# A two-layer encoder kernel with dense expert products: fewer tokens in the dense V product, more row groups, a shorter top-k table and a product moved to ScalarE

## The chip, the cores and the metric

One core of one Trainium2 chip. Its engines run side by side: TensorE (PE in the profile; PEld is its weight load), VectorE (DVE), ScalarE (ACT), GpSimd (POOL) and the DMA queues, which SyncE (SP) and POOL feed. The metric is the device time of one execution in microseconds, and the median of several.

## The reference

A trunk of two layers over 272 tokens (256 and 16 meta tokens), 1024 wide, all in float32. Layer 0 mixes tokens with a gated recurrence, layer 1 with a convolution. After each mixer comes the channel mixer that this document is about: per layer 16,384 experts with a row of U and a row of V each, of which every token uses 8 heads x 16.

```python
def peer_block(xc, w_query, sub_keys, expert_u, expert_v):
    q = (xc @ w_query).reshape(c, PEER_HEADS, 2, PEER_HALF)
    scores = jnp.einsum('chpk,pnk->chpn', q, sub_keys.astype(q.dtype))
    s1, i1 = lax.top_k(scores[:, :, 0], PEER_TOPK)
    s2, i2 = lax.top_k(scores[:, :, 1], PEER_TOPK)
    cand = (s1[..., :, None] + s2[..., None, :]).reshape(c, PEER_HEADS, PEER_TOPK * PEER_TOPK)
    s, flat = lax.top_k(cand, PEER_TOPK)
    ...
    g = jax.nn.softmax(s.astype(jnp.float32), axis=-1).astype(xc.dtype)
    act = jax.nn.gelu(jnp.einsum('chkd,cd->chk', expert_u[expert], xc))
    return jnp.einsum('chk,chkd->cd', g * act, expert_v[expert])
```

16 keys of 128 are picked on each of two axes, their 256 sums are made, and the best 16 sums are the experts. The last layer normalization drops the meta tokens, so layer 1 works on 256 tokens.

## The kernel before

**Dense, not gathered.** For most tokens `peer` computes all 16,384 experts: 128 tiles of U (128 experts each) times the tokens, GELU, a weight that is zero for experts that the token did not pick, and 128 tiles of V. `DENSE_U` gives the tokens for which U is dense (240 in both layers), `DENSE_V` those for which V is (208 and 192). Each loaded tile (512 KB, `raw`) is split into a rounded part `hi` (ScalarE, `load_split`, L159) and the rest `lo` (VectorE or POOL, L168), and a U tile is 24 matmuls in three passes: hi by the tokens' high part, hi by their low part, lo by the high part (`linears`, L196; tile `xs`). A V tile is eight matmuls by hi on both parts of the weights at once (L797) and eight by lo (L801).

**Few groups.** The other tokens are worked in groups of 16, which are 16 tokens x 8 heads = 128 rows. For pick k, `few_rows` gathers one row per partition by an indirect DMA from POOL's queue; `few_mult` takes the dot with x on VectorE, `few_add` adds a weighted row of V to `few_out`. A group outside DENSE_U needs 16 dots and 16 row sums (`EARLY`, `LATE`). A `DRAWN` group lies inside DENSE_U: POOL copies its dense results to a table in DRAM (`few_dump`) and fetches the picked ones (`few_draw`). At the end of a group TensorE adds `few_out` to the V sums (L843, 16 records). `near` groups take their expert positions from the main selection by way of DRAM (`few_spread`, `few_fetch`, on SP's queue); the group at 256 has a selection of its own (`few_topk`, in layer 0 alone).

**Stages of a layer.** First the query products and the scores, then:
- U, tiles 0 to 63 (`u_store` per tile). Meanwhile VectorE selects: 16 keys per axis and head, the table `cand`, the best 16 of it, positions, one-hot look-up of the keys (`topk_steps`). The tokens from 128 on are selected first. The selection of tokens 0 to 127 (`slow`) runs up to its heads' scans right behind, and its last eight steps between U tiles. POOL makes lo for tiles below `LO_FROM` = 34, VectorE from there. From `DOTS_FROM` = 41 on, 14 dots of the early group.
- U, tiles 64 to 127, with the gates (`u_out`). Chunks of 8 tokens: `one_hot` builds, on VectorE, a one-hot matrix of the first key (A) and of the second key times the high and the low half of the softmax weight (Bh in place, and Bl); `g_unit` multiplies them on TensorE (16 matmuls, L722 and L723) into the weights of all experts, and `weigh` multiplies these into the stored GELUs. Row groups go on: 2 dots, 8 row sums.
- V, 128 tiles. `few_plan` spreads the remaining row operations over tiles 4 to 112 by costs (3 for a row of an early group, 2 for the others); 72 row operations in layer 0, 56 in layer 1.

The order on each engine is set by a scheduler that keeps each engine's program order except where `issue_after` pins an instruction behind another. The buffers: lo 2, raw 4 and hi 2, and one `spare` that serves raw or hi (`self.fifth`).

Of the kernel before, what the change touches and what calls it, by code (L numbers as in the profile page):

```python
# [64 lines left out]
class Trunk:  # L65
# [514 lines left out]
    def peer(self, layer, n, xs):  # L580
# [10 lines left out]
        with tc.tile_pool(name=f"few{layer}", bufs=1) as kp:  # L591
            iT = ip.tile([HK, n // HC, 2, HC, 2], F16, name="iT")
            ghT = ip.tile([HK, n, 2], F16, name="ghT")
            glT = ip.tile([HK, n, 2], F16, name="glT")
            act_a = ap0.tile([P, JA, nu], F32, name="act_a")

            with tc.tile_pool(name=f"top{layer}", bufs=1) as sp:
# [7 lines left out]
                early, late, drawn = ([self.few_new(kp, layer, t0) for t0 in g[layer]] for g in (EARLY, LATE, DRAWN))  # L605
                near = [few for few in early + late + drawn if few["t0"] < 2 * P]
                for c0, md in ctiles:
# [8 lines left out]
                    if c0:  # L616
                        picked.append((c0, md, *self.topk(sp, sc, P)))
                        for few in early + late:
                            self.few_turn(sp, few, xs)
# [9 lines left out]
                def u_store(j, ps):  # L629
                    self.fifth = True  # L630
                    if j == LO_FROM:
                        with tc.issue_after(self.last_load):
                            self.few_load(kp, early[0], "kept")
                    behind = [few for few in early if few.get("left")]
                    if j >= LO_FROM and behind:
                        with tc.issue_after(self.dve_lo.ins):
                            for _ in range(min(2, behind[0]["left"])):
                                self.few_picked(behind[0])
                    elif j >= LO_FROM and len(picked[-1]) == 2:
# [38 lines left out]
            with tc.tile_pool(name=f"act1{layer}", bufs=1) as ap1:  # L678
# [16 lines left out]
                def one_hot(c0):  # L695
                    pairs = [HK, HC, NK // 2, 2]

                    def spread(t):
# [5 lines left out]
                    nc.vector.tensor_tensor(AB.rearrange("p x c (a b) -> p (x c) a b", b=2), keys,  # L704
# [758 lines left out]
```

## Time and profile before

| | us |
|---|---|
| median of 3 runs (1751.38 to 1758.8) | 1755.71 |
| the profiled execution | 1746.11 |
| its span | 1744.3 |
| layer 0: U 0 to 63, gates, V | 172.8, 350, 547 to 860 |
| layer 1: U 0 to 63, gates, V | 1055, 1231, 1428 to 1733 |

The last two rows give where in the span the stages begin, read from TensorE's timeline. A matmul's duration in the profile overlaps the next one's, so a tile's time is the distance between starts. In the timelines a bracket gives the idle time before an instruction and who ended it.

### The profile page before, as it was taken

Reading aid. Unit: us, or ns where it says so; the run is one execution under the profiler, and the core shown is the slowest. Engines: PE = TensorE matmul, PEld = TensorE weight load, DVE = VectorE, ACT = ScalarE, POOL = GpSimd, SP = SyncE. Lnnn points to the kernel's source line nnn. Section 1 sums busy time; section 2 is a strip of 40 time slices with the busy share of each in tenths; the row PEclk is TensorE's granted clock in tenths of the full one; section 3 lists DMA queues with packets and bytes.
Section 4 is the critical chain, followed back from the end, with each engine's and each line's share of the span. In section 5 each row is a group of like instructions: output and inputs, shape, how many; then the busy total and the mean of one; then the engine's idle time right before and its main releaser. Section 6 shows DMA issues by size and latency. Waiting matters only on the chain.

```text
span 1744.3 us, 34681 instructions
## 1 busy us (share of the span) xinstructions
PE 1716.3 (98%) x13436; PEld 1673.5 (96%) x13436; DVE 1507.6 (86%) x2818; ACT 899.6 (52%) x1491; POOL 616.1 (35%) x422
## 2 busy tenths in 40 slices
PE   8999999999999999999999999999999999999997
PEld 7899999999999999999989899999999999999997
DVE  7785998899997899988689869978889988889876
ACT  5553544554445555786542545445454455555553
POOL 1101892210202556752000017932102217777410
PEclk9999999999999999999999999999999999999999
DMA  5536667876757999998632356579767669999984
GB/s 206 169 134 183 182 198 262 299 236 194 228 183 232 340 360 373 364 373 322 208 122 72 121 175 170 182 254 318 243 191 221 219 202 326 335 363 353 344 310 153
DMA packets 126022, 423.83 MB, mean 243 GB/s; under 512 B 20768, under 2 KB 21920, under 8 KB 125728
## 3 DMA queue, kind: packets, MB, share of 16 engines
q1 hardware_dynamic: 96272, 324.04, 56.5%
q0 software_dynamic: 29584, 97.58, 15.2%
q8 instruction: 105, 1.72, 0.4%
q14 instruction: 61, 0.50, 0.1%
HBM read 411.35 MB, written 10.20 MB: 242 GB/s over the span
## 4 chain that ended last, share of the span: by engine, by line
PE 47%; DVE 3%; ACT 1%; DMA 0%; POOL 0%; issue 0%; DVEq 0%; ACTq 0%; POOLq 0%; SPq 0%
PE u L196 22%; PE acc L797 11%; PE acc L801 7%; PE u L243 3%; PE cv L1337 2%; PE g L722 1%; PE g L723 1%; DVE lo L168 0%; PE pre L263 0%; PE sps L613 0%; PE acc L843 0%; PE var L932 0%; DMA raw<-pw 0%; POOL lo L168 0%; ACT hi L159 0%
## 5 line engine op out<-in xcount | busy, mean ns | idle before, releaser
L159 ACT ACTIVATE hi<-raw 128x1024 fp32r<-128x1024 f32 x554 | 586.5, 1059 | 566.7 <-PE acc L797 241.9
L168 DVE TENSOR_TENSOR lo<-raw,hi 128x1024 fp32r<-128x1024 f32 x486 | 594.0, 1223 | 142.7 <-ACT hi L159 140.7
L196 PE MATMUL u<-xs,hi 128*128 128x240 f32 (+2 forms) x4544 | 569.0, 277 | 0.7 <-DVE xs L415 0.6
L196 PEld LDWEIGHTS u<-xs,hi 128*128 128x128 f32 x4544 | 537.6, 189 | 1.8 <-DVE xs L415 1.0
L797 PE MATMUL acc<-w,hi 128*128 128x416 f32 (+1 forms) x1952 | 401.2, 347 | 0.9 <-ACT hi L159 0.9
L797 PEld LDWEIGHTS acc<-w,hi 128*128 128x128 f32 x1952 | 339.8, 189 | 2.2 <-ACT hi L159 1.0
L1092 POOL DMA_INDIRECT rows<-peer_v,ids x128 | 203.0, 1586 | 313.1 <-DVE few_out L1133 168.9
L196 PE MATMUL u<-xs,lo 128*128 128x240 f32 (+2 forms) x2272 | 307.7, 276 | 4.1 <-POOL lo L168 4.0
L196 PEld LDWEIGHTS u<-xs,lo 128*128 128x128 f32 x2272 | 280.7, 189 | 6.0 <-POOL lo L168 5.6
L801 PEld LDWEIGHTS acc<-w,lo 128*128 128x128 f32 x2016 | 262.6, 191 | 0.9
L801 PE MATMUL acc<-w,lo 128*128 128x208 f32 (+1 forms) x2016 | 263.2, 272 | 0.0
L168 POOL TENSOR_TENSOR lo<-raw,hi 128x1024 fp32r<-128x1024 f32 x68 | 176.9, 2622 | 103.6 <-PE u L196 72.0
L1133 DVE SCALAR_TENSOR_TENSOR few_out<-rows,act,few_out 128x1024 f32<-128x1024 f32 x120 | 153.8, 1281 | 5.5 <-DMA rows<-peer_v,ids 5.4
L1092 POOL DMA_INDIRECT rows<-u_rows,ids x48 | 61.2, 1276 | 177.6 <-DVE rows L1099 134.1
L1109 POOL DMA_INDIRECT act<-own,turn x80 | 111.2, 1391 | 27.5 <-issue 18.6
L243 PE MATMUL u<-x,raw 128*128 128x272 f32 x480 | 114.1, 398 | 5.1 <-DMA x<-h 5.1
L243 PEld LDWEIGHTS u<-x,raw 128*128 128x128 f32 x480 | 92.5, 193 | 24.5 <-DMA raw<-w_in 5.1
L729 ACT ACTIVATE act_b<-g 128x488 f32<-128x488 f32 (+39 forms) x50 | 19.4, 389 | 116.9 <-DVE act_b L691 91.7
L407 POOL TENSOR_SCALAR xs<-x,par 128x272 fp32r<-128x272 f32 (+1 forms) x4 | 3.5, 878 | 180.5 <-DVE x L393 180.5
L704 DVE TENSOR_TENSOR AB<-iota,iT 128x2048 f16<-128x2048 f16 x50 | 61.1, 1225 | 0.0
L1099 DVE SCALAR_TENSOR_TENSOR rows<-rows,wide 128x1024 f32<-128x1024 f32 x48 | 58.5, 1219 | 1.1 <-DMA rows<-u_rows,ids 0.9
L778 POOL COPY own<-act_b 128x512 f32<-128x512 f32 (+2 forms) x15 | 14.6, 979 | 120.5 <-ACT act_b L740 94.3
(301 smaller groups left out, 1807.7 us busy)
## 6 DMA issues: line engine op xcount, KB each, us to landing
raw<-peer_u SPq DMA_DIRECT2D x256, 512.0 KB, 4.2
raw<-peer_v SPq DMA_DIRECT2D x248, 512.0 KB, 6.2
raw<-w_query SPq DMA_DIRECT2D x28, 512.0 KB, 3.8
raw<-pw SPq DMA_DIRECT2D x22, 512.0 KB, 3.5
raw<-w_in SPq DMA_DIRECT2D x16, 512.0 KB, 4.3
raw<-w_out SPq DMA_DIRECT2D x8, 512.0 KB, 3.9
raw<-peer_v SPq DMA_DIRECT2D x16, 256.0 KB, 4.5
own<-own POOLq DMA_DIRECT2D x15, 256.0 KB, 4.8
```

The lines of the kernel that those rows point to most:

```text
L159: self.act_hi = nc.scalar.activation(hi, raw, AF.Copy).ins
L168: i = e.tensor_tensor(lo[:, s], raw[:, s], hi[:, s].bitcast(F32), op=OP.subtract)
L196: self.mm = nc.tensor.matmul(ps[:, :n], l[:, k, :], xs(k, r)[:, :n], start=start, stop=stop)
L243: self.mm = self.nc.tensor.matmul(ps[:, :n], raw[:, k, :], x[:, k, :n], start=k == 0, stop=k == NB - 1)
L704: nc.vector.tensor_tensor(AB.rearrange("p x c (a b) -> p (x c) a b", b=2), keys, iT[:, c0 // HC].rearrange("p x c b -> p (x c) b")[:, :, N ...
L797: self.mm = nc.tensor.matmul(acc[b][:, :2 * n].rearrange("p (a t) -> p a t", a=2), hi, w[:, :, :n], start=j == 0, stop=j == NK - JG - 1, s ...
L801: self.mm = nc.tensor.matmul(main[b][:, :n], hi if p_ else lo, w[:, i, :n], start=False, stop=j == NK - 1 and not p_, skip_group_check=True)
L1092: self.last_rows = self.nc.gpsimd.indirect_dma_start(out=t, out_offset=None, in_=table, in_offset=bass.IndirectOffsetOnAxis(ap=few["ids"][ ...
L1099: self.nc.vector.scalar_tensor_tensor(t, t, 1.0, few["x"], op0=OP.mult, op1=OP.mult, accum_out=few["act"][:, k:k + 1])
L1109: self.nc.gpsimd.indirect_dma_start(out=few["act"][:, k:k + 1], out_offset=None, in_=few["table"].rearrange("p j (t o) -> (p j t) o", o=1) ...
L1133: nc.vector.scalar_tensor_tensor(few["out"], t, w, few["out"], op0=OP.mult, op1=OP.add)
L1337: nc.tensor.matmul(ps[:, :m], diag[i, b, k], h[j][:, s + k:s + k + m], start=(i, j, k) == steps[0], stop=False)
```

## The change

1. `DENSE_U` becomes (240, 224) and `DENSE_V` (192, 176). In both layers there are two early groups (240 and 256 in layer 0, 240 and 224 in layer 1) and three drawn ones; `LATE` goes. 80 tokens in layer 0 and 80 in layer 1 now have V from rows (64 before).
2. U tiles 0 to 63 hold 22 dots (from tile 29), the gate stage the other 10, all 16 row sums of the first early group and 4 of the second; V has 60 row operations in each layer. The first group's sum goes to DRAM and comes back in V (`few_spill`, `reload`). The rows of the gate stage alternate between a buffer of their own and `spare`, so raw has 4 buffers there.
3. VectorE takes lo from tile 25. The last eight steps of `slow` are at the tiles in `SLOW`.
4. `cand` keeps the sums of the first 4 keys with all 16 and of the other 12 with the first 4: 112. Four more small operations turn a place in it into the two positions. The look-up adds in a tree instead of a reduction.
5. Bl is made by ScalarE, one instruction per token with a scale per partition, and the A and B matrices of a chunk are built right behind the gate before.

```diff
-DENSE_U, DENSE_V = (240, 240), (208, 192)
-EARLY, LATE, DRAWN = ((256,), (240,)), ((240,), ()), ((224, 208), (224, 208, 192))
-DOTS_FROM, DOTS, ROWS, AHEAD, LO_FROM = 41, 14, 8, 2, 34
+DENSE_U, DENSE_V = (240, 224), (192, 176)
+EARLY, DRAWN = ((240, 256), (240, 224)), ((224, 208, 192), (208, 192, 176))
+DOTS_FROM, DOTS, ROWS, AHEAD, LO_FROM = 29, 22, 4, 2, 25
+SLOW = (25, 26, 27, 28, 30, 32, 34, 36)
+NEAR = 4
...
-SPREAD = 21
+SPREAD = 18
...
-        hi = self.stream("hi", F32R, 2, not self.fifth)
+        hi = self.stream("hi", F32R, 2, self.fifth is False)
...
-                    nc.vector.tensor_tensor(Bl_, Bh_, spread(glT), op=OP.mult)
-                    nc.vector.tensor_tensor(Bh_, Bh_, spread(ghT), op=OP.mult)
+                    for c in range(HC):
+                        nc.scalar.activation(Bl[:, c], Bh[:, c], AF.Copy, scale=glT[:, c0 + c:c0 + c + 1])
+                    hot["gate"] = Bh.rearrange("p c (a b) -> p c a b", b=2), ghT[:, c0:c0 + HC, None, :].to_broadcast(pairs)
...
+                    Bh_, gates = hot.pop("gate")
                     with tc.issue_after(second[0]):
-                        one_hot(c0)
+                        nc.vector.tensor_tensor(Bh_, Bh_, gates, op=OP.mult)
...
+                    if c0 + CC < n:
+                        with tc.issue_after(i.ins):
+                            one_hot(c0 + CC)
...
+                ops = later + [(first, 1, k) for k in range(TOPK)] + [(second_, 1, k) for k in range(ROWS)]
+                for e, (few, i, k) in enumerate(ops):
+                    t = e * (NK - JA - 7) // len(ops) + (2 if i and few is second_ else 0)
+                    home = (rp, "rows") if e % 2 else (self.wp, "spare")
+                    at_tile(t, self.few_rows, home[0], few, i, k, 1, home[1], order=False)
+                    at_tile(t + 3, *((self.few_add, few, k, kp, "kept") if i else (self.few_mult, few, k)))
...
-        cand = sp.tile([P, H, K, K], F32, tag=f"cand{H}", name="cand", bufs=1)
-        nc.vector.tensor_tensor(cand[:m], sv[:m, :, 0, :, None].to_broadcast([m, H, K, K]),
-                                sv[:m, :, 1, None, :].to_broadcast([m, H, K, K]), op=OP.add)
+        cand = sp.tile([P, H, NEAR * K + (K - NEAR) * NEAR], F32, tag=f"cand{H}", name="cand", bufs=1)
+        for part, rows, cols in ((cand[:m, :, :NEAR * K], slice(0, NEAR), slice(0, K)),
+                                 (cand[:m, :, NEAR * K:], slice(NEAR, K), slice(0, NEAR))):
...
-            nc.vector.tensor_reduce(idx[:m].rearrange("p a h k -> p (a h) k")[:, g:g + w], oh[:m, g:g + w],
-                                    op=OP.add, axis=AX.X)
+            for o in (8, 4, 2):
+                nc.vector.tensor_tensor(oh[:m, g:g + w, :, :o], oh[:m, g:g + w, :, :o], oh[:m, g:g + w, :, o:2 * o], op=OP.add)
+            nc.vector.tensor_tensor(idx[:m].rearrange("p a h k -> p (a h) k")[:, g:g + w], oh[:m, g:g + w, :, 0],
+                                    oh[:m, g:g + w, :, 1], op=OP.add)
...
-        rows = [(few, i, k) for few in early + late + drawn for i in range(2)
-                for k in range((ROWS if few in early else 0) if i else 0 if few in late else TOPK, TOPK)]
+        first, second = early
+        rows = [(second, k) for k in range(ROWS, TOPK)] + [(few, k) for few in drawn for k in range(TOPK)]
```

VectorE's program in layer 0, where its selection ends and lo begins (`fi<-fv` are the scans of a head's sums; `lo` is that of U tile 34). Before:

```order
L970 MAX fv<-r_2076 128x8
L971 MAX_INDEX fi<-fv,r_2076 128x8
L168 TENSOR_TENSOR lo<-raw,hi 128x1024
L974 CAST s_3209<-si 128x32
L977 TENSOR_SCALAR pu<-fi 128x16
L978 TENSOR_SCALAR pu<-fi 128x16
L980 CAST pf<-pu 128x64
L987 TENSOR_TENSOR oh<-iota_98,pf 128x512
L168 TENSOR_TENSOR lo<-raw,hi 128x1024
```

And now, where this `lo` is that of tile 25 and the steps of `slow` follow (`far` and `pu` are the small operations on the places):

```order
L997 MAX fv<-r_2094 128x8
L998 MAX_INDEX fi<-fv,r_2094 128x8
L170 TENSOR_TENSOR lo<-raw,hi 128x1024
L1001 CAST s_2941<-si 128x256
L1006 TENSOR_SCALAR far<-fi 128x128
L1007 TENSOR_SCALAR pu<-fi 128x128
L1008 TENSOR_SCALAR far<-far 128x128
L1009 TENSOR_SCALAR pu<-fi 128x128
L1010 TENSOR_TENSOR pu<-pu,far 128x128
L1011 SCALAR_TENSOR_TENSOR pu<-pu,fi 128x128
L1013 CAST pf<-pu 128x512
L170 TENSOR_TENSOR lo<-raw,hi 128x1024
```

The first lo of VectorE still stands behind the last scan, but belongs to a tile nine earlier, and the main selection's steps come straight behind it.

VectorE in the gate stage of layer 0, one chunk: `act_a<-g` and `act_b<-g` are the weighings, `AB<-iota` the one-hots of the next chunk but one, `AB<-AB,ghT` the high product of the next. Before:

```order
L691 SCALAR_TENSOR_TENSOR act_a<-g,act_a 128x64x8
L691 SCALAR_TENSOR_TENSOR act_b<-g,act_b 128x24x8
L711 TENSOR_TENSOR Bl<-AB,glT 128x1024
L704 TENSOR_TENSOR AB<-iota,iT 128x2048
L712 TENSOR_TENSOR AB<-AB,ghT 128x1024
L168 TENSOR_TENSOR lo<-raw,hi 128x1024
L744 TENSOR_TENSOR act_b<-act_b,tmp 128x80
L168 TENSOR_TENSOR lo<-raw,hi 128x1024
```

And now:

```order
L699 SCALAR_TENSOR_TENSOR act_a<-g,act_a 128x64x8
L699 SCALAR_TENSOR_TENSOR act_b<-g,act_b 128x15x8
L1133 SCALAR_TENSOR_TENSOR rows,act_1625<-rows,wide 128x1024
L710 TENSOR_TENSOR AB<-iota,iT 128x2048
L726 TENSOR_TENSOR AB<-AB,ghT 128x1024
L170 TENSOR_TENSOR lo<-raw,hi 128x1024
L755 TENSOR_TENSOR act_b<-act_b,tmp 128x48
L170 TENSOR_TENSOR lo<-raw,hi 128x1024
L755 TENSOR_TENSOR act_b<-act_b,tmp 128x48
```

Bl is gone from VectorE; in this chunk a dot of a row group stands in its place, in others none.

ScalarE in the same stage (`act_b<-u` and `tmp` are the GELUs of a U tile). Before:

```order
L159 ACTIVATE hi<-raw 128x1024
L740 ACTIVATE act_b<-u 128x152
L743 ACTIVATE tmp<-u 128x88
L729 ACTIVATE act_b<-g 128x36x8
L159 ACTIVATE hi<-raw 128x1024
```

And now:

```order
L161 ACTIVATE hi<-raw 128x1024
L751 ACTIVATE act_b<-u 128x152
L754 ACTIVATE tmp<-u 128x88
L715 ACTIVATE Bl<-AB,glT 128x128 x8
L740 ACTIVATE act_b<-g 128x34x8
L161 ACTIVATE hi<-raw 128x1024
```

The eight low products of the next chunk stand between a tile's GELUs and the rest of the gate's weighing, ahead of the next hi.

More of the change, by code (lines that the diff above doesn't have):

```diff
@@ L604, in peer @@
                 picked = []
-                early, late, drawn = ([self.few_new(kp, layer, t0) for t0 in g[layer]] for g in (EARLY, LATE, DRAWN))
-                near = [few for few in early + late + drawn if few["t0"] < 2 * P]
+                early, drawn = ([self.few_new(kp, layer, t0) for t0 in g[layer]] for g in (EARLY, DRAWN))
+                near = [few for few in early + drawn if few["t0"] < 2 * P]
+                dots = [(few, 0, k) for few in early for k in range(TOPK)]
+                dots, later = dots[:DOTS], dots[DOTS:]
                 for c0, md in ctiles:
@@ L617, in peer @@
                         picked.append((c0, md, *self.topk(sp, sc, P)))
[L618 removed]
+                        for few in early:
                             self.few_turn(sp, few, xs)
@@ L630, in u_store @@
                     self.fifth = True
-                    if j == LO_FROM:
+                    if j in (LO_FROM, SLOW[-1]):
                         with tc.issue_after(self.last_load):
-                            self.few_load(kp, early[0], "kept")
+                            self.few_load(*((sp, early[0], "turned") if j == LO_FROM else (kp, early[1], "kept")))
                     behind = [few for few in early if few.get("left")]
[L635 to L639, printed above, removed]
+                    if j in SLOW:
                         with tc.issue_after(self.dve_lo.ins):
@@ L789, in peer @@
                 vp = row_pool.__enter__()
-                self.few_plan(kp, vp, early, late, drawn, scale)
+                self.fifth = True
+                self.few_plan(kp, vp, early, drawn, scale)
                 acc = [self.bank(NB - 1 - b, f"acc{b}") for b in range(NB)]
@@ L1111, in few_draw, with few_spill @@
             in_offset=bass.IndirectOffsetOnAxis(ap=few["turn"][:, k:k + 1], axis=0))
-    def few_gelu(self, few, last):
-        self.nc.scalar.activation(few["act"], few["act"], AF.Gelu_apprx_tanh)
-        if last:
-            self.warm(AF.Abs_reciprocal_sqrt)
+    def few_spill(self, few):
+        few["sum"] = self.dp.tile([P, D], F32, name=f"sum{few['layer']}_{few['t0']}")
+        self.nc.gpsimd.dma_start(few["sum"], few["out"])
     def few_load(self, pool, few, tag):
@@ L1142, in few_plan, with reload @@
         begin = 4
         slots = len(rows) + ahead
-        cost = list(accumulate(3 if few in early else 2 for few, _, _ in rows + rows[-1:] * ahead))
+        cost = list(accumulate(3 if few is second else 2 for few, _ in rows + rows[-1:] * ahead))
         at = [begin + (c - cost[0]) * (NK - 4 * JG - begin) // cost[-1] for c in cost]
+        def reload():
+            first["out"] = vp.tile([P, D], F32, tag="wide", name="few_out", bufs=1)
+            with self.tc.issue_after(self.last_load):
+                self.nc.sync.dma_start(first["out"], first["sum"])
@@ L1147, in step @@
         def step(s):
-            if s == ahead and not late:
+            if s == ahead:
                 self.warm(AF.Abs_reciprocal_sqrt)
             if s >= ahead:
-                few, i, k = rows[s - ahead]
-                if i == 0:
-                    self.few_mult(few, k)
-                    if k == TOPK - 1:
-                        self.few_gelu(few, few is late[-1])
-                else:
-                    if k == 0:
-                        self.few_weigh(few, scale)
-                    self.few_add(few, k, *few["home"])
-                    if k == TOPK - 1:
-                        self.sums.append((at[s] + 4, few))
@@ L1162, in step @@
-            if s < len(rows):
-                few, i, k = rows[s]
-                if i == 0 and "loaded" not in few:
-                    few["loaded"] = self.few_load(vp, few, "wide")
-                few["rows"][k] = self.few_rows(vp, few, i, k, ahead + 1)
-        self.steps = [(t, lambda s=s: step(s)) for s, t in enumerate(at)]
+                few, k = rows[s - ahead]
+                if k == 0:
+                    self.few_weigh(few, scale)
+                self.few_add(few, k, *few["home"])
@@ L1173, in few_plan @@
         self.steps.sort(key=lambda s: s[0])
-        self.sums = []
+        self.sums = [(begin + 1, first)]
     def few_step(self, j):
```

111 lines of the change are left out of this document (63 added, 48 removed).

## The prediction

> **What bounds the kernel now.** I read the page's busy shares and chain first, then the windows by stage, then single tiles in the timelines.
>
> ```profile
> PE 1716.3 (98%) x13436; PEld 1673.5 (96%) x13436; DVE 1507.6 (86%) x2818; ACT 899.6 (52%) x1491; POOL 616.1 (35%) x422
> PE 47%; DVE 3%; ACT 1%; DMA 0%; POOL 0%; issue 0%; DVEq 0%; ACTq 0%; POOLq 0%; SPq 0%
> ```
>
> TensorE is busy 98% of the span and is nearly all of the chain that names an engine. The stages (columns: stretch, length, busy PE, PEld, DVE, ACT, POOL, clock, DMA share, GB/s) are, for each layer, the first half of U, the second half of U with the gates, and V:
>
> ```profile
> 176.00:352.00 176.00, 173.84 (x1540) 172.75 (x1539) 163.07 (x466) 88.79 (x140) 102.16 (x49) 1.00 0.74 238
> 352.00:546.00 194.00, 193.47 (x1919) 192.50 (x1918) 182.69 (x267) 94.16 (x215) 25.02 (x23) 1.00 0.65 207
> 548.00:848.00 300.00, 298.98 (x1997) 296.43 (x1996) 260.76 (x280) 192.10 (x290) 154.19 (x108) 1.00 0.94 343
> 1056.00:1233.00 177.00, 174.79 (x1548) 173.60 (x1547) 155.71 (x451) 88.17 (x138) 100.89 (x49) 1.00 0.74 237
> 1233.00:1426.00 193.00, 192.75 (x1892) 191.52 (x1891) 177.55 (x257) 93.70 (x212) 35.82 (x31) 1.00 0.67 211
> 1428.00:1720.00 292.00, 292.00 (x2054) 291.83 (x2053) 244.73 (x267) 156.71 (x162) 163.05 (x110) 1.00 0.93 330
> ```
>
> TensorE bounds all six at full clock, but two helpers stand close: VectorE in the gate stages (182.69 of 194, 177.55 of 193) and the DMA engines in V (0.94, 0.93). So TensorE time saved counts only until one of them binds.
>
> **The change part by part.**
>
> *V with 16 tokens fewer.* One V tile is eight matmuls by hi and eight by lo; layer 0 (208 tokens) and layer 1 (192):
>
> ```profile
> 641.25 1.70 PE L797 MATMUL acc<-w,hi 128*128 128x416 f32 x8
> 642.78 1.04 PE L801 MATMUL acc<-w,lo 128*128 128x208 f32 x8
> 1442.29 1.59 PE L797 MATMUL acc<-w,hi 128*128 128x384 f32 x8
> 1443.71 1.03 PE L801 MATMUL acc<-w,lo 128*128 128x192 f32 x8
> 1444.58 1.59 PE L797 MATMUL acc<-w,hi 128*128 128x384 f32 x8
> 1497.49 1.72 PE acc L843 x16
> ```
>
> Starts count, not durations. The eight hi take 642.78 - 641.25 = 1.53 us at 416 columns and 1.42 at 384. The eight lo take 1444.58 - 1443.71 = 0.87 at 192, or 109 ns each. The sums of row groups (L843, last row) take 107.5 ns each although they stream 16 columns. So near 108 ns something other than the columns sets a matmul with such weights, and only the hi matmuls go on shrinking, 0.11 us per tile. Layer 0 gets what layer 1 has now, 0.11 and 0.01 from lo, times 124 tiles: -14.8 us. Layer 1 gets 0.11 x 124 = -13.6.
>
> *The fifth row group per layer* costs one more L843 row each: 2 x 1.72 = +3.4.
>
> *U in layer 1 with 224 columns.* A U tile is 24 matmuls:
>
> ```profile
> 267.47 1.96 PE L196 MATMUL u<-xs,hi 128*128 128x240 f32 x16
> 269.26 1.06 PE L196 MATMUL u<-xs,lo 128*128 128x240 f32 x8
> 270.16 1.96 PE L196 MATMUL u<-xs,hi 128*128 128x240 f32 x16
> 1024.40 2.05 PE L196 MATMUL u<-xs,hi 128*128 128x256 f32 x16
> 1027.24 2.05 PE L196 MATMUL u<-xs,hi 128*128 128x256 f32 x16
> ```
>
> 240 columns take 2.69 us, 112.1 ns each; 256 take 2.84. Linear, 224 would save 0.15 x 128 tiles = 19 us; at a floor it saves nothing. 224 lies nearest to 240, and under it stand 109 and 107.5, so I take 110.3: 1.8 ns x 3072 = -5.5 (0 to -19).
>
> *Gates.* Two chunks of eight tokens fewer per layer, and layer 1 turns one group more (16 wide_ps matmuls ahead of U):
>
> ```profile
> 479.35 0.23 PE L722 MATMUL g<-AB 128*128 128x128 f16 x1
> 480.23 0.36 PE L196 MATMUL u<-xs,hi 128*128 128x240 f32 x1
> L1038 PE MATMUL wide_ps<-eye,xs 128*16 128x128 f32 x48 | 3.8, 228 | 0.4 <-ACT turned L1040 0.4
> ```
>
> A chunk holds TensorE for 0.88 us: 4 x 0.88 = -3.5. The turn is a third of 3.8: +1.3.
>
> *Top-k over 112 sums, and lo on VectorE from tile 25 instead of 34.* POOL makes lo while VectorE selects; then VectorE takes over, behind its last selection.
>
> ```profile
> L967 DVE MAX8 fv<-cand 128x8 f32<-128x256 f32 x33 | 13.3, 411 | 0.1
> L952 DVE MAX8 sv<-sc 128x8 f32<-128x128 f32 x66 | 18.2, 280 | 3.0 <-ACT sc L615 3.0
> L959 DVE TENSOR_TENSOR cand<-sv 128x2048 f32<-128x2048 f32 x4 | 12.5, 3124 | 0.0
> L977 DVE TENSOR_SCALAR pu<-fi 128x128 uint32<-128x128 uint32 x4 | 1.9, 485 | 0.0
> 265.22 1.23 DVE L168 TENSOR_TENSOR lo<-raw,hi 128x1024 fp32r<-128x1024 f32 x1 [1.08 <-ACT hi L159]
> 1147.70 1.22 DVE L168 TENSOR_TENSOR lo<-raw,hi 128x1024 fp32r<-128x1024 f32 x1 [6.44 <-ACT hi L159]
> 1151.75 1.06 PE L196 MATMUL u<-xs,lo 128*128 128x240 f32 x8
> ```
>
> 128 sums fewer save 0.131 us per scan, 144 save 0.147; five scans per head: 0.74. Layer 0 has 17 heads ahead of its takeover (12.6), layer 1 16 (11.8). The table shrinks to 896 of 2048 sums, -1.75 twice, and about -1 for the lone group of layer 0. Four new small operations cost 4 x 0.485 = 1.9. Adding 3840 elements in a tree instead of reducing 4096 I take as equal. So VectorE is free 15 us earlier in layer 0, 13.5 in layer 1. But it is wanted nine tiles earlier, 24.2 us. The slack now: in layer 0 it is free at 264.14 and the lo pass of that tile starts at 269.26, less 1.28 for lo: 3.8; in layer 1 1141.26 against 1151.75: 9.2. Stalls: 24.2 - 15 - 3.8 = 5.4 and 24.2 - 13.5 - 9.2 = 1.5. Together +6.5 (0, if the scans shrink more or VectorE, beside POOL for less time, runs faster; +14, if the small operations wait as long again). On SP the position DMAs move three tiles (8.1 us) earlier, while the selection that they wait for is ready about 7 us earlier; the loads behind them wait as now, 7 us, covered by the loaded-ahead tiles:
>
> ```profile
> SPq L1069 <- DVE sv L952: 7.0, 1, 7.0
> ```
>
> Later in U the 22 dots take 0.75 x 1.22 of each 2.69 us tile beside lo's 1.23, so 80%: hidden by TensorE.
>
> *Gate stage.* Rows for VectorE and ScalarE:
>
> ```profile
> L711 DVE TENSOR_TENSOR Bl<-AB,glT 128x1024 f16<-128x1024 f16 x50 | 34.1, 683 | 0.0
> L1133 DVE SCALAR_TENSOR_TENSOR few_out<-rows,act,few_out 128x1024 f32<-128x1024 f32 x120 | 153.8, 1281 | 5.5 <-DMA rows<-peer_v,ids 5.4
> L704 DVE TENSOR_TENSOR AB<-iota,iT 128x2048 f16<-128x2048 f16 x50 | 61.1, 1225 | 0.0
> L691 DVE SCALAR_TENSOR_TENSOR act_a<-g,act_a 128x512 f32<-128x512 f32 x50 | 34.1, 682 | 0.0
> 730.23 0.97 ACT L1241 ACTIVATE diag<-ident,w_lo 128x128 fp32r<-128x128 f32 x3
> ACT act_b L729 <- DVE act_b L691: 91.7, 38, 4.6
> ```
>
> VectorE loses Bl (26 x 0.68 = 17.7 in layer 0, 16.4 in layer 1) and two chunks (each AB 1.23, the high product 0.68, two weighings 1.1: 6.0), and gains 20 rows of about 1.25 (10 to 30): +25. It then has 184 of 192.2 us in layer 0 and 180 of 188.5 in layer 1. The eight low products go to ScalarE, of the shape of diag: 0.97 for three, so 0.29 apart and 2.4 for eight. They fit into its wait for VectorE's weighing (91.7 us in 38 places), so ScalarE costs nothing by itself; were that gone, hi would be late by up to 2.4. But the in-place high product waits for them. After a gate, VectorE weighs (1.1) and makes the next AB (1.2), 2.2 by starts, against 2.5: 0.3 us of waiting where no row operation stands between, in half of the chunks, and lo is queued behind it. That is 4 us per layer; and the last four tiles have no chunk, so 5 us there are of no use to the rest. VectorE is over by about 1 us in each layer; unevenness may double or treble it. I take +3 each, +6 (0 to +16).
>
> *V's transfers.* By the plan's costs a drawn row comes every 1.59 tiles in both layers (1.38 and 1.74 before):
>
> ```profile
> raw<-peer_v SPq DMA_DIRECT2D x248, 512.0 KB, 6.2
> 648.00:668.00 20.00, 20.00 (x136) 19.87 (x136) 17.96 (x22) 12.35 (x14) 11.45 (x8) 1.00 1.01 379
> 728.00:748.00 20.00, 20.00 (x134) 19.86 (x133) 19.77 (x25) 17.55 (x38) 14.31 (x13) 1.00 1.00 376
> ```
>
> With 0.524 MB per V tile and per gathered row, a tile needs 1.63 x 0.524 = 0.854 MB. Layer 0 asks for 0.854 / 2.29 = 373 GB/s, what it draws now. Layer 1 asks for 0.854 / 2.18 = 392, and 376 to 379 stood at a full share. At 373 to 376 a tile takes 2.28 instead of 2.18 over the 76 tiles of the drawn rows: 7.6 us, less what the loaded-ahead tiles cover. I take +5 (0 to +8); POOL's longer list of draws has room (163 of 292 us).
>
> **Sum:** -14.8 - 13.6 + 3.4 - 5.5 - 3.5 + 1.3 + 6.5 + 6 + 5 = -15.2 us. The profiled execution took 1746.1 and would take 1731; the median of the runs shown is 1755.7, 9.6 above it, and becomes 1740.5, which I predict.
>
> **The rivals.** *All new work stays hidden* (no handoff stall, no gate or DMA limit): 15.2 + 17.5 = -32.7, 1723. For it: TensorE idles nowhere now with VectorE at 94%. Against: the slack of 3.8 us is read from one row.
>
> *U shrinks linearly*: 13.5 us more, 1727. Against it stand the lo rows at 109 ns. The Trainium skill (TensorE: Matmul & The Clock Gate, section Back-to-back issue gap) gives N/2.4 + 2.5 ns for an isolated matmul, which would be this case, -20 for U; its section on LDWEIGHTS, columns/1.2, gives 107 ns, with which the 107.5 agrees.
>
> *VectorE waits for ScalarE in every chunk (slower).* If a low product takes 0.5 us instead of 0.29, eight take 4.0 and the high product waits 1.8 where no row stands between and 0.6 where one does: 46 chunks, 55 us, of which 5 fit into slack. 1740.5 - 6 + 50 = 1785. It decides from about 0.42 each. Against: the three diags at 0.29.
>
> *The transfers and VectorE cost their upper bounds*: +16, +8, +14 instead of 17.5 gives 1761; two of the three, 1753: no change.
>
> *A lower DMA ceiling.* If what V's transfers can get is no more than layer 0's mean over the whole V stage, 343 GB/s, a drawn tile takes 2.49 us in both layers: 15 more in layer 0, 24 instead of 5 in layer 1, 1775. The rows above show 376 and 379, so it gets 2 in 100. The Trainium skill (DMA: Bandwidth & Descriptors, section Where 436 GB/s comes from) names about 358 GB/s as what binds from HBM, by which the sum would be 1758; the trace disagrees with that figure by its 376 and 379.
>
> **How the numbers follow.** Half a per cent, 8.8 us, is about what a measurement of this kernel tells from no change. My sum has 0.45 (own range 1732 to 1747, nearly all faster), all hidden 0.18, linear U 0.05, upper bounds 0.20 (no change, a fifth of it slower), low ceiling 0.02 (slower), VectorE waiting for ScalarE 0.10, which covers its smaller forms. Faster 0.65, same 0.22, slower 0.13. The range 1722 to 1759 leaves about a tenth on each side.
>
> **What will show it.** V tiles at 2.29 and 2.18 us, U tiles of layer 1 at 2.65; a TensorE gap of some 5 us before tile 25 of U in layer 0; the high product idle before itself on ScalarE by 0.3 us; DMA share 1.00 and V tiles of 2.2 to 2.3 late in layer 1. A gate stage longer than 196 us, or a low product over 0.4 us, makes the prediction wrong.

## The result and the profile after

The changed kernel takes 1767.85 us (median; 1759.17 to 1774.34) against 1753.53 of the kernel before: 1.0077 times as long, 95% interval 1.0048 to 1.0106 (eight runs of each). The forecast was 1740.5 and faster, with a range of 1722 to 1759. The profiled execution took 1771.5 us against 1746.1, 25.4 more. The page's busy shares, the chain by engine, and the granted clock in 40 slices:

```profile
PE 1704.0 (96%) x13420; PEld 1662.2 (94%) x13420; DVE 1533.1 (87%) x2906; ACT 1000.7 (57%) x1858; POOL 696.9 (39%) x480
PE 6%; DVE 1%; DVEq 0%; issue 0%
PEclk9999979999999999999999999899999899999999
```

TensorE is busy 12 us less than before in a span that is 25 us longer: it waits now. The chain reaches back only into V of layer 1. The clock, which had no dip, has one in slice 6 (221 to 265 us) and smaller ones later. By stage (first half of U, gates, V, per layer; columns as in the prediction):

```profile
173.00:368.00 195.00, 179.56 (x1545) 178.41 (x1545) 180.58 (x542) 88.82 (x142) 90.49 (x47) 0.95 0.70 235
368.00:572.00 204.00, 198.53 (x1922) 197.38 (x1922) 187.90 (x264) 151.51 (x408) 77.00 (x53) 0.98 0.78 262
572.00:869.00 297.00, 294.92 (x2063) 294.39 (x2061) 249.59 (x271) 193.59 (x294) 167.40 (x124) 0.99 0.93 333
1071.00:1259.00 188.00, 175.38 (x1544) 174.19 (x1543) 172.34 (x493) 87.89 (x140) 91.33 (x47) 0.97 0.74 249
1259.00:1463.00 204.00, 196.85 (x1891) 195.68 (x1891) 182.20 (x256) 145.55 (x390) 76.17 (x53) 0.97 0.78 258
1463.00:1745.00 282.00, 281.01 (x2058) 280.23 (x2057) 245.55 (x269) 153.83 (x161) 161.38 (x114) 1.00 0.95 348
```

From the first tile of a stage to that of the next, in us:

| | U 0 to 63 | gates | V (first to last full tile) | between, and both ends |
|---|---|---|---|---|
| layer 0 before, after | 176.53, 194.96 | 198.01, 204.05 | 305.64, 295.16 | |
| layer 1 before, after | 176.71, 188.11 | 196.40, 203.84 | 289.33, 280.75 | |
| difference, both layers | +29.8 | +13.5 | -19.1 | +1.2 |

V gave what was counted on. U and the gates took it back, and more. What TensorE waits for (engine line, releaser: us in total, times, longest), then what SP's queue waits for ahead of the position transfers:

```profile
PE u L198 <- ACT hi L161: 19.2, 4, 8.9
PE u L198 <- DVE lo L170: 12.0, 4, 4.7
PE g L730 <- DVE AB L726: 5.8, 2, 4.8
```

```profile
SPq L1104 <- DVE sv L978: 19.7, 1, 19.7
SPq L1104 <- DVE sv L975: 19.0, 1, 19.0
```

SP comes to the position transfers three tiles sooner than before, but the selection is not ready: 19.7 us instead of 7.0. The tile loads are queued behind. In layer 0 ScalarE then has no tile to round (first row), TensorE idles 8.9 us, and what follows runs at half speed (TensorE's timeline):

```profile
235.00 1.06 ACT L161 ACTIVATE hi<-raw 128x1024 fp32r<-128x1024 f32 x1 [15.09 <-DMA raw<-peer_u]
```

```profile
226.02 1.16 PE L198 MATMUL u<-xs,lo 128*128 128x240 f32 x8 [0.35 <-POOL lo L170]
236.11 3.77 PE L198 MATMUL u<-xs,hi 128*128 128x240 f32 x16 [8.93 <-ACT hi L161]
239.68 1.91 PE L198 MATMUL u<-xs,lo 128*128 128x240 f32 x8
...
244.58 1.96 PE L198 MATMUL u<-xs,hi 128*128 128x240 f32 x16
...
262.04 2.06 PE L198 MATMUL u<-xs,lo 128*128 128x240 f32 x8 [4.73 <-DVE lo L170]
```

The second wait, at 262, is the takeover at tile 25: VectorE's last scan has just ended. In the gate stage the worst place, on VectorE, POOL and TensorE:

```profile
494.42 1.28 DVE L1160 SCALAR_TENSOR_TENSOR few_out<-rows,act,few_out 128x1024 f32<-128x1024 f32 x1 [6.41 <-DMA rows<-peer_v,ids]
```

```profile
484.04 1.73 POOL L773 COPY own<-act_b 128x512 f32<-128x512 f32 x1 [3.93 <-DMA own<-own]
486.07 0.57 POOL L774 DMA_DIRECT2D own<-own  x1 [0.30 <-POOL own L773]
486.94 1.01 POOL L1127 DMA_INDIRECT rows<-peer_v,ids  x1 [0.30 <-DVE lo L170]
```

```profile
496.36 0.27 PE L730 MATMUL g<-AB 128*128 128x128 f16 x1 [4.76 <-DVE AB L726]
```

POOL waits for its one copy buffer (three copies of dense results fall due at tiles 31, 33 and 35), a gather stands behind the copy, VectorE's row operation waits 6.4 us for the gather, and the high product that TensorE needs stands behind the row operation.

### The profile page after: what moved, and what is told of

Same layout as the page of the kernel before. It is cut to its first block, busy times and chain, and to the rows that moved or that the text cites. A ratio compares the mean times of both kernels' runs of the same rounds, so it can differ in the third digit from the quotient of the medians.

```text
span 1769.7 us, 35319 instructions
## 1 busy us (share of the span) xinstructions
PE 1704.0 (96%) x13420; PEld 1662.2 (94%) x13420; DVE 1533.1 (87%) x2906; ACT 1000.7 (57%) x1858; POOL 696.9 (39%) x480
## 5 line engine op out<-in xcount | busy, mean ns | idle before, releaser
L198 PE MATMUL u<-xs,hi 128*128 128x224 f32 (+3 forms) x4544 | 576.4, 279 | 19.9 <-ACT hi L161 19.2
L820 PE MATMUL acc<-w,hi 128*128 128x384 f32 (+1 forms) x1952 | 377.4, 335 | 1.9 <-ACT hi L161 1.9
L1127 POOL DMA_INDIRECT rows<-peer_v,ids x160 | 274.3, 1714 | 247.6 <-DVE few_out L1160 131.5
L198 PE MATMUL u<-xs,lo 128*128 128x224 f32 (+3 forms) x2272 | 309.9, 278 | 15.6 <-DVE lo L170 12.0
L198 PEld LDWEIGHTS u<-xs,lo 128*128 128x128 f32 x2272 | 283.1, 192 | 17.6 <-DVE lo L170 12.7
L824 PE MATMUL acc<-w,lo 128*128 128x192 f32 (+1 forms) x2016 | 262.3, 271 | 1.0 <-DVE turn L1136 1.0
L1160 DVE SCALAR_TENSOR_TENSOR few_out<-rows,act,few_out 128x1024 f32<-128x1024 f32 x150 | 192.8, 1286 | 23.0 <-DMA rows<-peer_v,ids 22.6
L170 POOL TENSOR_TENSOR lo<-raw,hi 128x1024 fp32r<-128x1024 f32 x50 | 130.9, 2632 | 124.0 <-PE u L198 72.8
L1127 POOL DMA_INDIRECT rows<-u_rows,ids x64 | 87.0, 1359 | 229.9 <-DVE rows L1133 160.9
L715 ACT ACTIVATE Bl<-AB,glT 128x128 f16<-128x128 f16 x368 | 112.7, 389 | 28.0 <-PE g L731 23.5
L730 PE MATMUL g<-AB 128*128 128x128 f16 x368 | 48.0, 224 | 5.8 <-DVE AB L726 5.8
```

Source lines behind the costliest of these rows:

```text
L170: i = e.tensor_tensor(lo[:, s], raw[:, s], hi[:, s].bitcast(F32), op=OP.subtract)
L198: self.mm = nc.tensor.matmul(ps[:, :n], l[:, k, :], xs(k, r)[:, :n], start=start, stop=stop)
L715: nc.scalar.activation(Bl[:, c], Bh[:, c], AF.Copy, scale=glT[:, c0 + c:c0 + c + 1])
L820: self.mm = nc.tensor.matmul(acc[b][:, :2 * n].rearrange("p (a t) -> p a t", a=2), hi, w[:, :, :n], start=j == 0, stop=j == NK - JG - 1, s ...
L824: self.mm = nc.tensor.matmul(main[b][:, :n], hi if p_ else lo, w[:, i, :n], start=False, stop=j == NK - 1 and not p_, skip_group_check=True)
L1127: self.last_rows = self.nc.gpsimd.indirect_dma_start(out=t, out_offset=None, in_=table, in_offset=bass.IndirectOffsetOnAxis(ap=few["ids"][ ...
```

## The experiments

The theory: **the selection is late**. The new steps made it longer, not shorter, and two things that wait for it had been moved to earlier tiles. The rivals: SP's wait alone; the takeover alone; and for the gates, VectorE's load. Times are medians; a ratio is to the kernel before on the same chip (1750.9 to 1752.8), taken from all runs, so not quite the quotient of the medians. The experiments ran on three chips, so ratios are what to compare between them. Stage times and stalls come from one profiled run each, and "U takes" gives tiles 0 to 63 of layer 0 and of layer 1.

**1. Position transfers back at tile 21.**

```diff
-SPREAD = 18
+SPREAD = 21
```

> The changed kernel with the position transfers at tile 21 again (SPREAD 18 to 21), nothing else. Late selection (my theory): the selection of tokens 128 to 271 ends at 228.1 us whatever SP does, and VectorE's last scan at 261, so SP's waits for it fall by three tiles, from 19.7 and 19.0 us to about 11.5 each, TensorE's first stall from 8.9 and 8.7 to about 1, but TensorE then comes to tile 25 some 11 us sooner while VectorE is no sooner free: the stall there grows from 4.7 to 13 to 16 in layer 0 and from 2.1 to 10 to 13 in layer 1. Time 1760 to 1768, within 8 of the changed kernel. SP alone (rival): the second stall was only an aftermath of the first; both layers get back 11 to 13 us each, time 1743 to 1747.

1772.08, ratio 1.0136 (1.0104 to 1.0167). SP waits 14.1 and 9.5 us. TensorE's timeline in layer 0:

```profile
240.03 3.77 PE L198 MATMUL u<-xs,hi 128*128 128x240 f32 x16 [4.53 <-ACT hi L161]
262.80 2.06 PE L198 MATMUL u<-xs,lo 128*128 128x240 f32 x8 [10.04 <-DVE lo L170]
```

The first stall halves, the second doubles; U takes 195.4 and 192.1. SP alone is out. The time lies above the 1760 to 1768 that I expected, and above the changed kernel's ratio. Nor was the split as I expected (1 and 13 to 16), since the positions came at 232.05 instead of 228.14: without the long stall POOL works on, and the selection gets slower (experiments 5 and 6).

**2. VectorE's lo from tile 31, transfers still at 18.**

```diff
-DOTS_FROM, DOTS, ROWS, AHEAD, LO_FROM = 29, 22, 4, 2, 25
-SLOW = (25, 26, 27, 28, 30, 32, 34, 36)
+DOTS_FROM, DOTS, ROWS, AHEAD, LO_FROM = 35, 20, 2, 2, 31
+SLOW = (31, 32, 33, 34, 36, 38, 40, 42)
```

> The changed kernel with VectorE taking lo from tile 31 instead of 25 (the last steps of slow and the dots move with it, 20 dots and 2 row sums instead of 22 and 4), position transfers still at tile 18. Late selection: the first stall stays (8.9 and 8.7 us idle, and half clock behind it), the stall at the takeover goes (4.7 and 2.1 idle with 2.3 and 0.3 of slow clock): 7 us in layer 0 and 2.4 in layer 1, time about 1758. Handoff alone (rival): U 0 to 63 goes back to 177 us in both layers, 30 us less, time 1738. SP alone: no change, 1767.

1766.08, ratio 1.0092. The takeover's stall is gone, the first stands at 8.97 and 8.65; U takes 188.1 and 187.3 (188 and 185.7 expected). The takeover alone is out. The time is 8 us over the 1758 expected: V of layer 1, with two rows more, took 288.7 (280.75 in the changed kernel). With the same rows it took between 283 and 293 in later runs, which no run here explains.

**3. Both.** Experiment 2 with the transfers at tile 22.

> Position transfers at tile 22 and VectorE's lo from tile 31, both at once. Late selection: neither stall is left, SP waits 7 to 9 us as before the change (7.0), U 0 to 63 takes 177 in layer 0 and 176 in layer 1, against 195.0 and 188.1: 30 us less, time about 1738, granted clock 0.99. If the small operations of the selection are what is late for another reason (each waits for a running lo of POOL, which then makes lo without a pause), VectorE is free after tile 31 needs it and a stall of 1 to 4 us is left at tile 31: 1740 to 1744. SP alone: as the first of these, 1744. Handoff alone: as the second, 1738.

1752.71 (1744.49 to 1764.49), ratio 1.0021 (1.0001 to 1.0042): within half a per cent of before, but not the 1738. In the profiled run, which was the fastest (1744.49), U takes 183.2 and 176.4. Layer 1 is clean. In layer 0 stalls of 1.79 and 2.16 us are left, since the positions are ready at 232.28 (225.37 before the change) and VectorE's last scan ends at 265.5 (264.1 before).

**4. The copies of the gate stage spread out,** U untouched.

```diff
-12 * g + 6 * i + 3
+10 * g + 5 * i + 3
```

> The changed kernel with the copies of the dense results to the table spread out in the gate stage (12 g + 6 i + 3 becomes 10 g + 5 i + 3, so that none lies less than three tiles ahead of another), the U half untouched. Gathers behind the copies on POOL (my theory): POOL's waits of 3.3 and 3.9 us for the one copy buffer go, the gathers behind them leave 6 us sooner, VectorE's longest wait for a row falls from 6.5 to under 2, the one long stall of each gate stage (9.24 and 10.99 us tiles, and half clock behind) goes: gate stages 197 instead of 204.05 and 195 instead of 203.84, time about 1752. VectorE saturated (rival, the prediction's own term): VectorE has 188 and 182 us of work in these 204 and a smaller stall stands elsewhere instead; stages 201 or more, time 1763 or more.

1761.56, ratio 1.0071 (1.0054 to 1.0088). The profiled gate stages take 198.0 and 197.0, as expected, with VectorE busy 187.6 us in the first (187.9 without the edit), so its load alone does not make a stage of 204. U is as in the changed kernel (194.4 and 187.0). But the ratio is hardly under the changed kernel's 1.0077, and I had expected 1752. The long wait for a gather falls on some stages and not on others: without this edit a stage took 197.8 in experiment 1 and 195.3 in experiment 8, with it one took 205.1 (experiment 9). So the waits explain what those 204 us are made of, but that spreading the copies saves time is not shown.

**5. One reduction instead of the tree,** on top of 3.

```diff
-            for o in (8, 4, 2):
-                nc.vector.tensor_tensor(oh[..., :o], oh[..., :o], oh[..., o:2 * o], op=OP.add)
-            nc.vector.tensor_tensor(idx[...], oh[..., 0], oh[..., 1], op=OP.add)
+            nc.vector.tensor_reduce(idx[...], oh[...], op=OP.add, axis=AX.X)
```

> Position transfers at tile 22, VectorE's lo from tile 31, and the look-up adds by one reduction again instead of the tree of four additions. In the kernel with both moves the four additions took 3.19, 2.67, 2.71 and 2.59 us in layer 0, and 0.69 and 0.61 for the last two in the changed kernel, where POOL stood still. VectorE waits for POOL's running lo (my theory): each separate operation loses up to a lo of POOL (2.4 us), one reduction loses it once: 4.4 instead of 11.2, the selection is ready at 225.5 instead of 232.3, SP's waits fall from 9.8 and 6.2 to about 3 and 0, VectorE's last scan ends at 257 instead of 263, no stall in U of layer 0 (183.2 to 177). Time 5 to 7 less than with both moves: 1746. The additions cost what their elements cost (rival): as the prediction had it, the reduction of 4096 takes as long as the 3840 additions, no change, 1752.

1740.88, ratio 0.9932 (0.9908 to 0.9956). U takes 175.3 and 174.7. The look-up's additions on VectorE in layer 0: in experiment 3, in the changed kernel (its last two), and the reduction here:

```profile
220.61 3.19 DVE L1030 TENSOR_TENSOR oh<-oh 128x2048 f16<-128x2048 f16 x1
223.98 2.67 DVE L1030 TENSOR_TENSOR oh<-oh 128x1024 f16<-128x1024 f16 x1
226.77 2.71 DVE L1030 TENSOR_TENSOR oh<-oh 128x512 f16<-128x512 f16 x1
229.67 2.59 DVE L1031 TENSOR_TENSOR idx<-oh 128x256 f32<-128x256 f16 x1
```

```profile
226.64 0.69 DVE L1030 TENSOR_TENSOR oh<-oh 128x512 f16<-128x512 f16 x1
227.50 0.61 DVE L1031 TENSOR_TENSOR idx<-oh 128x256 f32<-128x256 f16 x1
```

```profile
220.68 4.39 DVE L1029 TENSOR_REDUCE idx<-oh 128x256 f32<-128x4096 f16 x1
```

The duration does not follow the elements: 2048, 1024, 512 and 256 take 3.2 to 2.6 us. In the changed kernel the last two take a quarter, where POOL stood still (TensorE's stall). With POOL at work each takes about as long as one of POOL's lo (2.40). The reduction takes 4.39 with POOL at work.

**6. POOL makes each lo in two halves,** on top of 3.

```diff
-FULL if j >= LO_FROM else (("p", 1024),)
+FULL if j >= LO_FROM else (("p", 512),) * 2
```

> Position transfers at tile 22, VectorE's lo from tile 31, the tree kept, and POOL makes each lo in two halves of 512 columns. VectorE waits for POOL's running lo: with pieces half as long the waits are halved, the additions of the tree take 1.3 to 1.9 each instead of 2.6 to 3.2, the selection is ready 4 to 6 us sooner (227 to 228), U of layer 0 some 4 us shorter, time about 1748, unless POOL's second instruction per tile costs more than the 0.29 us that it has left of each 2.69, in which case TensorE waits for lo in every tile below 31 and the kernel is slower. The additions are slow by themselves, by their strided operands (rival): they stay at 2.6 to 3.2, no change, 1752.

1749.12, ratio 0.9970. The same additions, on VectorE:

```profile
215.87 1.55 DVE L1030 TENSOR_TENSOR oh<-oh 128x1024 f16<-128x1024 f16 x1
217.53 1.58 DVE L1030 TENSOR_TENSOR oh<-oh 128x512 f16<-128x512 f16 x1
219.28 1.49 DVE L1031 TENSOR_TENSOR idx<-oh 128x256 f32<-128x256 f16 x1
```

Nothing about VectorE's instructions changed, only the length of POOL's, and they fall by 1.1 us. So each of these additions waits for the POOL instruction that runs, and the wait follows that instruction's length. U takes 177.8 and 177.1.

**7. The kernel before with the shorter table alone** (112 sums, small operations, tree).

> The kernel before with the shorter table alone (112 sums, small operations, tree), nothing else. By the prediction's terms VectorE is free 15 us sooner and the time is that of before (TensorE bounds), 1751. Late selection: scans save 11 to 12 us of VectorE's work, but the split table, the small operations and the tree, each behind a lo of POOL, give it back ahead of the positions: the selection is ready at 232 instead of 225.4, SP's wait at tile 21 grows from 7.0 to 14, TensorE stalls 3 to 5 us in layer 0 and 0 to 4 in layer 1 with half clock behind, takeover at tile 34 as good as before; time 5 to 10 more, 1756 to 1761.

1768.35, ratio 1.0086 (1.0057 to 1.0115): this part alone is slower by as much as the whole change, where the prediction's terms give no change and I had expected 1756 to 1761. VectorE's last scan in layer 0 ends at 264.19 instead of 264.14: nothing of the 15 us is left. The positions are ready at 232.03 instead of 225.37, SP waits 14.1 and 13.9, TensorE idles 3.90 and 4.80, U takes 183.5 and 184.1 (176.5 and 176.7): 14.4 us. V of layer 0 took 7 more as well, in waits of VectorE that no run here explains.

**8. The changed kernel with one reduction alone.**

> The changed kernel with one reduction instead of the tree and nothing else: position transfers stay at tile 18, lo from tile 25, copies as they were. The tree alone is the cause in U (rival): the selection is 7 us sooner, both stalls of U go, 30 us less, 1738 plus nothing for the gates that stay as they are. Places that count on a selection which does not exist (my theory): with the reduction the positions are ready at 225, still 17 after SP comes to them at 208.4, so SP waits 16.5 to 17 us in both layers instead of 19.7 and 19.0; TensorE's first stall falls from 8.9 and 8.7 to about 5 or 6, still long enough for the half clock; VectorE's last scan ends at 256 to 258, TensorE wants its first lo some 10 us sooner, a stall of 3 to 6 us. U 0 to 63 takes 187 to 190 and 182 to 185 instead of 195.0 and 188.1, the gate stages 198 to 204 as they fall: time 1755 to 1762.

1760.82, ratio 1.0063. SP still waits 16.5 and 13.9; stalls of 6.32 and 4.73 in layer 0, 5.15 and 2.12 in layer 1; U takes 191.7 and 183.9. Both layers' U 0 to 63 together: 383.1 in the changed kernel, 375.6 here, 359.6 with the two places alone (experiment 3), 350.0 with both (experiment 5). The tree alone is out: tiles 18 and 25 count on a selection that is sooner still.

**9. All four mends:** 3, 4 and 5 together.

> The changed kernel with position transfers at tile 22, VectorE's lo from tile 31, one reduction instead of the tree, and the copies of the gate stage spread out. If the four causes are all: U 0 to 63 takes 177 and 176, the gate stages 198 and 196, V 296 and 284; the sum is 1735 to 1738 for the profiled run and 1738 to 1742 in the median, 0.5 to 0.7 per cent under before (1751), which is the forecast less its takeover and gate terms. If VectorE's load in the gate stage is a bound of its own (rival), those stages stay at 200 and the time at 1745 to 1750.

1736.55 (1727.07 to 1747.26), ratio 0.9909 (0.9881 to 0.9938). U takes 175.3 and 174.9. Of the gate stages layer 1's takes 195.1, but layer 0's still 205.1. There, on POOL and on VectorE:

```profile
438.13 6.07 POOL L773 COPY own<-act_a 128x512 f32<-128x512 f32 x1
...
445.38 5.66 POOL L1125 DMA_INDIRECT rows<-peer_v,ids  x1 [0.31 <-issue]
```

```profile
456.77 1.28 DVE L1158 SCALAR_TENSOR_TENSOR few_out<-rows,act,few_out 128x1024 f32<-128x1024 f32 x1 [6.58 <-DMA rows<-peer_v,ids]
```

**10. The copies on ScalarE,** on top of 9.

```diff
-                    with tc.issue_after(self.last_rows):
-                        nc.gpsimd.tensor_copy(own, act[...])
-                    nc.gpsimd.dma_start(few["table"][:, j:j1], own)
+                    with tc.issue_after(self.act_hi):
+                        nc.scalar.activation(own, act[...], AF.Copy)
+                    with tc.issue_after(self.last_rows):
+                        nc.gpsimd.dma_start(few["table"][:, j:j1], own)
```

> All four mends, and the copies of the dense results to the table's buffer are made by ScalarE, so that POOL has only transfers left in the gate stage. With the four mends one such copy of 0.61 us took 6.07 on POOL and the gather behind it another 5.66, VectorE waited 6.58 for the row and TensorE 4.5 (gate stage of layer 0: 205.1 instead of 198). POOL's copies wait behind VectorE's row operations (my theory): with no copy there, gate stages of 196 to 198 and 194 to 196, VectorE's longest wait for a row in the gate stage under 3, time 1727 to 1732 with a smaller spread. The gathers themselves are held up (rival): the one of 5.66 us stays, stages of 200 to 205 now and then, 1735 to 1738.

1732.30 (1730.25 to 1737.06), ratio 0.9880 (0.9858 to 0.9902): the best version, 20 us under the kernel before. VectorE's waits for rows of V:

```profile
DVE few_out L1159 <- DMA rows<-peer_v,ids: 20.0, 22, 1.9
```

None is longer than 1.9 us. The gate stages take 200.8 and 195.0, and the runs lie within 7 us instead of 20. In layer 0 I had expected 198 at most. The rival is not quite out: with no copy on POOL, the issue of a gather still took up to 4.99 us. The gain over experiment 9 (0.9880 against 0.9909) lies within the intervals; the shorter waits and the smaller spread are what shows.

**11. The low one-hot product back on VectorE,** on top of 9.

> All four mends (position transfers at tile 22, lo from tile 31, one reduction, copies spread out), and the low one-hot product is back on VectorE (one operation per chunk, 0.68 us, as before the change). VectorE saturated (the prediction's term): it had 187.6 of 198 and 181.3 of 197 us of work in the gate stages; 24 and 22 products add 16 and 15, so it needs 204 and 196 and more with the unevenness; gate stages 206 to 210 and 199 to 203, against 195 to 200 with undisturbed gathers: time 1746 to 1755. ScalarE's product is a wait that VectorE is better without (the prediction's slower rival): stages the same or shorter, 1730 to 1737.

1750.61, ratio 0.9979 (0.9958 to 1.0000). The gate stages take 212.2 and 198.3 (columns: PE, PEld, DVE, ACT, POOL, clock, DMA):

```profile
348.00:560.00 212.00, 201.29 (x1920) 198.35 (x1920) 200.26 (x291) 93.39 (x216) 96.70 (x54) 0.98 0.76 249
1234.00:1432.00 198.00, 194.09 (x1888) 192.30 (x1887) 192.39 (x280) 92.74 (x214) 83.93 (x53) 1.00 0.81 266
```

In experiment 9 the stages took 205.1 and 195.1, the first with the same wait of 6.6 us for a row as here. VectorE is now busy 200.3 and 192.4 us in them, some 13 and 10 more, and they are 7.1 and 3.2 longer. By the medians, giving the product to ScalarE is worth 14 us at this load.

**12. The table of 256 sums,** on top of 3 and 4.

> Position transfers at tile 22, lo from tile 31, copies spread out, and the table of all 256 sums with its two small operations and the reduction, as before the change. What the shorter table is worth once its additions are one operation: five scans of 16 heads get longer by 0.147 each (11.8 us, half of it ahead of the positions), the small operations shorter by 4.3, the split table by 1.4 twice. The positions are ready about 226 (224.5 with the short table), VectorE's last scan ends at 263 to 264 instead of 258, TensorE wants lo of tile 31 from 259: a stall of 3 to 5 us with half clock behind it in layer 0, 0 to 2 in layer 1; time 1741 to 1746. If the short table is worth nothing (rival), 1737 as with it.

1746.61, ratio 0.9971. VectorE's first lo starts at 263.64 instead of 258.22, TensorE stalls 4.00 there, and U takes 182.2 and 175.9. Against experiment 9, the short table with its additions in one operation is worth some 8 us in U; with the tree it cost 14 in the kernel before (experiment 7).

## Why the prediction was wrong, point by point

| term | forecast | measured |
|---|---|---|
| V, with the fifth groups and the DMA limit: layer 0, layer 1 | -13.1, -6.9 | -10.5, -8.6 |
| U of layer 1 at 224 columns | -5.5 | -1.3 |
| four gate chunks, one turn | -3.5, +1.3 | -3.5, +1.2 |
| takeover of lo, with SP's wait | +6.5 | +30.5 |
| gate stage | +6 | +17.6 |
| sum | -15.2 | +25.4 |

The measured terms are the stage differences of the two profiled runs. The chunks and the 224 columns are taken out of the stages where they lie, the chunks at the forecast's 0.88 us each, and the 1.2 of the turn is all that lies between the stages and at both ends.

**The step that failed** is "VectorE is free 15 us earlier", and with it "the selection that they wait for is ready about 7 us earlier". The scans did shrink (0.41 to 0.26 us each). But three other terms ate it up in layer 0. The small operations, put at 1.9 more, take 5.8 instead of 1.5, 4.3 more. The tree, which the prediction took as equal, takes 11.2 instead of 4.39. And the split table, put at 1.75 less for each selection, takes longer: 2.00 + 2.23 and 2.09 + 2.31 us in two operations, where one took 2.84 and 3.93, 1.9 more. Together that is 13 us, as much as the 12.6 that the scans were to save. In experiment 3, where POOL runs through, the positions are 7 us later (232 against 225.4), and VectorE is free at 265.5, not at 249; in the changed kernel, where the long stall stops POOL, it is 228.1 and 260.9. From experiment 3, three of the small operations and one of the scans:

```profile
203.54 2.42 DVE L1006 TENSOR_SCALAR far<-fi 128x128 uint32<-128x128 uint32 x1
205.88 0.22 DVE L1007 TENSOR_SCALAR pu<-fi 128x128 uint32<-128x128 uint32 x1
206.48 2.49 DVE L1011 SCALAR_TENSOR_TENSOR pu<-pu,fi 128x128 uint32<-128x128 uint32 x1
220.43 0.27 DVE L997 MAX8 fv<-r 128x8 f32<-128x112 f32 x1
```

The first and the last small operation met a running lo of POOL; the four between them fell into a pause of 0.46 us before POOL's next lo and take 0.2 to 0.3. A scan takes 0.27 beside POOL and 0.26 without.

The mechanism, a stall at the takeover, was named. Its size came from durations that held little of this waiting: the 0.485 of a small operation is the mean of one that took 1.29 and three of 0.21 or 0.22. The bound of +14 ("if the small operations wait as long again") was too low, because it let only the small operations wait. SP's wait, for which the prediction has "as now, 7 us", became 19.7 and 19.0, and the stalls behind it, 8.9 and 8.7 us, took the larger part. (The two stalls forecast, 5.4 and 1.5, add up to 6.9, not 6.5; nothing hangs on it.)

The Trainium skill (SBUF — State Buffer, section Who interferes with whom) says that VectorE and GpSimd share one port pair, which one of them holds for a whole instruction, that a VectorE operation with two SBUF inputs contends with a GpSimd instruction that reads SBUF, and that a reduction never does. The traces agree: 2.6 us against 0.61 for the same addition, 1.5 with POOL's pieces halved, 4.39 for the reduction beside a busy POOL. By it, the swap of a reduction for additions speaks against the change. I did not weigh it.

**Half clock.** Each long stall cost more than its idle time, which no term held: after 8.93 us of idling the next two tiles took 5.27 and 3.20 instead of 2.69. The Trainium skill (TensorE: Matmul & The Clock Gate, section What's actually happening) puts the array at half rate after an idle window of about 3.4 us. Granted clocks of 0.50 stood after the waits of 8.9 and 4.7, none after the one of 2.11 in layer 1. But 0.73 and 0.70 stood in the two stretches of 3 us behind one of 1.88 in V of layer 0, and 0.52 in the 3 us behind one of 2.16 in experiment 3. So shorter waits were followed by a lower clock too, not each time, and no run here sets the limit.

**The gate stage.** VectorE's load was right (187.9 and 182.2 us busy; 184 and 180 forecast over stretches 3 to 4 us shorter than the stages), and experiment 11 shows that it has little room: the stages grow when it gets 10 to 13 us more. The low product was right too: eight take 2.45 us (2.4 forecast), and the high product waited for it twice, 2.8 us in all. So the rival of a wait in each chunk did not come. What was missed is POOL's queue: copies and gathers share it, and VectorE stands in order behind a gather. Without copies on POOL no such wait stands in the profiled run (experiment 10); why a gather itself is at times issued slowly stays open. The end of V in layer 0 lost 2.6 us where ScalarE waits 2.36 for the transfer of `xr`, which it copies ahead of hi.

**U at 224 columns** stands at a floor, higher than the 110.3 ns that I took:

```profile
1250.90 1.95 PE L198 MATMUL u<-xs,hi 128*128 128x224 f32 x16
1252.69 1.05 PE L198 MATMUL u<-xs,lo 128*128 128x224 f32 x8
1253.58 1.95 PE L198 MATMUL u<-xs,hi 128*128 128x224 f32 x16
```

1253.58 - 1250.90 = 2.68, or 111.7 ns each (112.1 at 240), so the linear rival did not come.

**V was right by the tile.** Tiles of 2.29 and 2.20 us (2.29 and 2.18 forecast); in layer 1:

```profile
1739.13 1.50 PE L820 MATMUL acc<-w,hi 128*128 128x352 f32 x8
1740.47 1.03 PE L824 MATMUL acc<-w,lo 128*128 128x176 f32 x8
1741.33 1.49 PE L820 MATMUL acc<-w,hi 128*128 128x352 f32 x8
```

The DMA limit cost at most 1.6 us, not 5; the longest single wait there, 0.98 us, was for VectorE's `turn`.

With the mends the kernel reaches 1736.55, close to the 1740.5 that the forecast gave, but this is in part chance. In the profiled run of experiment 9 V is 13.5 us shorter where 20.0 was forecast, and U 0 to 63 is 3.0 shorter where the forecast has it longer. The change pays once the steps of the selection are mended and nothing is placed ahead of it; as it was built, the selection that it leaned on was not there.

## What to carry to other kernels

A short addition, cast or integer operation of VectorE that met a running GpSimd instruction took 2.4 to 3.2 us here, about that instruction's length, whatever its own size, while a scan took 0.27 and the reduction 4.39. So count how often such an operation has to come in anew, not its elements, and read durations where GpSimd is busy. When a consumer is moved ahead, read when its producer ends in the trace, and where the same change alters that producer, work out its new end as a term of its own. A queue that serves two purposes (SP: positions and tiles; POOL: copies and gathers) turns one late item into a stall of everything behind it.

## What the hardware showed that was not expected

POOL is slowed too: a copy of 512 elements took 0.61 us or 6.07, and the issue of a gather 0.94 or 5.66, in a stage where VectorE is busy nearly all the time. Without copies on POOL a gather's issue still took up to 4.99 us (experiment 10). That VectorE's operations are what holds it is likely, but no run isolates it. ScalarE made the same copy in 0.61 to 0.64 every time. And V of layer 1 drew more than the 376 to 379 GB/s that the prediction took as the most at a full share (last two columns: DMA share and GB/s):

```profile
1540.00:1560.00 20.00, 20.00 (x150) 20.00 (x149) 17.73 (x20) 9.84 (x10) 14.45 (x11) 1.00 1.03 395
```
